# FFN output by seven products: three residual chunks loaded early, the last dual's sums in four parts

## The chip, the cores and the metric

The kernel runs on one core of a Trainium2 chip. The metric is the time of one execution on the device in microseconds. The times here are of that one core.

## The reference

One trunk layer on 1024 tokens of 1024 channels: a mixing sub-layer, then the feed-forward sub-layer (FFN), then a norm. The change lies in the FFN, where DFF is 2816:

```
h2 = rms_norm(x, norm_ffn_g[l]) * (1.0 + sc2) + sh2
a, bgate = jnp.split(jnp.einsum('bsd,df->bsf', h2, w_ffn_in[l]), 2, axis=-1)
x = x + g2 * jnp.einsum('bsf,fd->bsd', jax.nn.silu(a) * bgate, w_ffn_out[l])
...
return rms_norm(x, final_norm_g)
```

The product with `w_ffn_in` is called the FFN input below, the one with `w_ffn_out` the FFN output.

## The kernel before, in words

Activations are held transposed, channels on the 128 partitions and tokens along a row, in two halves of 512 tokens. Each float32 operand is split in a high part and the remainder (`th`, `tl` for activations, `wh`, `wl` for weights), and a product of two is three matmuls of 128x512 (`mm3`: lines 397, 398 and 400). A weight block lands in a `raw` buffer (line 218); ScalarE makes `wh` of it (line 234) and VectorE `wl` (line 235). There are three `wh` and three `wl` buffers, so that the cast for one product waits until TensorE is through with the product three places earlier. Of `raw` buffers there are six in this stage, in use in turn, and a load waits until the split of the block that lay there is done.

A 2x2 block product is made with seven products instead of eight (`PRODUCTS`, in the order 1, 2, 6, 5, 7, 3, 4). One such set of seven is called a **dual**. It needs sums of the four weight blocks (lines 254, 257, 259 and 301, on VectorE) and sums of the four blocks of the activation, and its results collect in three pairs of PSUM banks, x, y and z. In the z banks product 5 begins a sum, which is read out, and product 3 then adds to it.

The **FFN input** runs 11 duals. Each dual is followed by `hid_set`: from the four blocks of the activation it forms the seven operands of the FFN output, by four sums (lines 1336, 442, 1340 and 442), splits each in high and low (lines 437 on ScalarE and 438 on VectorE) and stores them to device memory. For the first ten duals they go through three `stage` buffers (line 1328), for the last dual through pairs of tiles called `hidh` and `hidl` (line 1324). Under each `in_product` of the last dual, `group_load` reads back the operands of group 0 for the product of the same number (line 1349), on the queue of GpSimd (POOL).

The **FFN output** takes the 11 operand sets in groups of 3, 4 and 4. For each group it runs two duals, d = 0 and d = 1, each for half of the output rows. A product of group 0 has 2 x 3 x 3 = 18 matmuls, one of groups 1 and 2 has 24. `out_evac` (line 1420, on VectorE) scales each bank and adds it to a chunk of the residual: chunk x1[j] holds 128 output channels of all tokens. Half d = 0 adds to chunks 0, 1, 4 and 5, half d = 1 to 2, 3, 6 and 7; the products 5, 7 and 4 to the later two of these (4 and 5, 6 and 7). The residual had been stored to device memory after the mixing sub-layer (`x1_dram`), and is loaded again: chunks 0 and 1 while the FFN input still runs, into buffers of their own (line 1408), the other six, in the order 4, 5, 2, 3, 6, 7, after the last dual's `hid_set` (line 1413), in the place that the `stage` buffers and the activation blocks (`gi`) held.

A scheduling layer sets the order of each engine's queue when the program is built, from the order of the code and its own estimate; on the chip each queue runs in order. DMAs of POOL's queue use eight semaphores in turn, so that each waits until the DMA eight places before it has landed.

Of the kernel before, what the change touches and what calls it, by code (L numbers as in the profile page):

```python
# [35 lines left out]
F32 = mybir.dt.float32  # L36
# [4 lines left out]
P = 128  # L41
D = 1024
T = 1024
H = 512
KC = D // P
# [86 lines left out]
def block_kernel(ctx: ExitStack, tc: tile.TileContext, x0, xT, c, vecs, ada, w_first, w_plain, w_duals,  # L132
                 w_short, w_conf, w_o, w_fi, w_fo0, w_fo1, outT):
    nc = tc.nc
# [4 lines left out]
    def open_pool(name, bufs, stack=None, **kw):  # L139

        p = tc.tile_pool(name=name, bufs=bufs, reuse_waits="tile", **kw)
        return p, (stack.enter_context(p) if stack else p.__enter__())

    def close(*pools):
        for p, _ in reversed(pools):
            p.__exit__(None, None, None)
# [27 lines left out]
    def g_tile(name):  # L174
        return gsp.tile([P, H], F32, tag="gs", name=name)
# [192 lines left out]
    def modulation(i, raw=None):  # L368

        if raw is None:  # L370
            raw = load(ada[i])
        else:
            nc.sync.dma_start(raw, ada[i])
        modulation_of(i, raw)
# [34 lines left out]
    def product(banks, m, t, evac=None, between=None, y_tile=ps2_tile, z_tile=ps_tile, onto=""):  # L409


        w = next_w()
        b = {"1": "x", "6": "x", "7": "x", "4": "x", "2": "y", "5": "z", "3": "z"}[m]
        n = len(t)
        for p in range(2):
            if (b, p) not in banks:
                banks[b, p] = {"x": ps_tile, "y": y_tile, "z": z_tile}[b](b)
            ps = banks[b, p]
            for k in range(n):
                c0 = (p * n + k) * P  # L420
                mm3([ps], slice(c0, c0 + P), w, [t[k]], m in "125" and m not in onto and k == 0, k == n - 1, m in "6734" + onto)
            if evac:
                evac(p, m, ps)
            if between and p == 0:
                between()
# [7 lines left out]
    def t_pair(name):  # L433
        return hl_tile(name + "h"), hl_tile(name + "l")

    def t_split(src, hi, lo):
        t_split.act = nc.scalar.copy(hi, src).ins  # L437
        t_split.ins = nc.vector.tensor_tensor(lo, src, f32(hi), ALU.subtract).ins  # L438

    def minus(out, a, b):  # L440

        nc.vector.scalar_tensor_tensor(out=out, in0=a, scalar=-1.0, in1=b, op0=ALU.mult, op1=ALU.subtract)
# [694 lines left out]
    for h in range(2):  # L1137
# [4 lines left out]
        for o in range(KC):  # L1142
            g = g_tile("gb")
# [9 lines left out]
    x1 = [None] * KC  # L1153
    x1_dram = [dram.tile([P, T], F32, name=f"x1_dram{j}") for j in range(KC)]
# [56 lines left out]
    def norm_2_sums(m):  # L1211

        b12, b22 = ([x1[k + i][:, halves[1]] for k in range(KH)] for i in (0, KH))
        b21 = [x1[k + KH][:, halves[0]] for k in range(KH)]
        with tc.issue_after(t_split.ins), tc.issue_after(t_split.act):
            for k in range(KH):
                if m == "7":
                    nc.vector.tensor_tensor(b12[k], b22[k], b12[k], ALU.subtract)
                elif m == "4":
                    minus(b21[k], t2[k], b21[k])  # L1220
            for k in range(KH):
                ts[m][k] = t_pair("t" + m)
                t_split({"5": x1[k][:, halves[0]], "7": b12[k], "3": b22[k], "4": b21[k]}[m], *ts[m][k])
        norm_2_sums.ins = t_split.ins

    N_IN = FC // 2
# [90 lines left out]
    def store(key, src):  # L1317

        hid_dram[key] = dram.tile([P, T], F32R, name="hid" + "_".join(map(str, key)))
        if key[0] == N_IN - 1:  # L1320
            hl = t_pair("hid")
            t_split(src, *hl)
            for t, s in zip(hl, halves):
                nc.gpsimd.dma_start(hid_dram[key][:, s], t)
            return
        s = stagep.tile([P, T], F32R, tag="stage", name="stage")
        t_split(src, s[:, :H], s[:, H:])
        nc.gpsimd.dma_start(hid_dram[key], s)  # L1328

    def hid_set(d):  # L1330

        (b11, b12), (b21, b22) = ((ha[2 * d + p, "4"], ha[2 * d + p, "6"]) for p in range(2))
        store((d, "1"), b11)
        store((d, "2"), b21)
        t2 = gip.tile([P, H], F32, tag="g", name="t2")
        nc.vector.tensor_tensor(b11, b11, b12, ALU.subtract)
        minus(t2, b11, b22)
        store((d, "6"), t2)
        store((d, "5"), b11)
        nc.vector.tensor_tensor(b12, b22, b12, ALU.subtract)  # L1340
        store((d, "7"), b12)
        store((d, "3"), b22)
        minus(b21, t2, b21)
        store((d, "4"), b21)

# [8 lines left out]
    def group_load(g, m):  # L1354
        to[g, m] = [t_load((FIRST[g] + i, m)) for i in range(GROUPS[g])]

    def in_product(d, m, between=None):
        late = EARLY[d] == 1
        if late and m == "2":
            for p in range(2):  # L1360
                in_evac(d)(p, "1", in_banks[d]["x", p])
        product(in_banks[d], m, ts[m], None if late and m == "1" else in_evac(d), between,
                z_tile=ps2_tile if d in (0, 2) else ps_tile)
        if d == N_IN - 1:
            group_load(0, m)
# [13 lines left out]
    for i, (d, m) in enumerate(in_order[5:]):  # L1379
        if i < 4:  # L1380
            norm_2_sums("5734"[i])
        elif i == 4:
            close(*phase_1)
            rawap = open_pool("raw_a", 1, side="right", stack=ctx)[1]
            raws.append(rawap)
            x1aps = [s2p, open_pool("x1a", 1, side="right", stack=ctx)[1]]
            phase_2 = [open_pool("gi", 7), open_pool("stage", 3, side="right")]
            gip, stagep = (p for _, p in phase_2)
        with ExitStack() as order:
            if d < 2:  # L1390
                order.enter_context(tc.issue_after(mm3.ins))
            in_product(d, m)
        if m == PRODUCTS[-1]:
            if 2 <= d < 6:
                with tc.issue_after(in_evac.ins):
                    for b in range(40 + 2 * (d - 2), 42 + 2 * (d - 2)):
                        modulation(b, x1aps[b % 2].tile([P, T], F32, tag="x1", name="ada"))
            if d:
                hid_set(d)
        elif (d, m) == (1, "6"):  # L1400
            hid_set(0)


    ng2 = cp.tile([P, KC], F32, name="ng2")
    nc.vector.tensor_scalar(ng2, mod[:, 40:48], -1.0, None, ALU.mult)
    x1 = [x1aps[j].tile([P, T], F32, tag="x1", name=f"x1{j}") for j in range(2)]
    for j in range(2):
        nc.gpsimd.dma_start(x1[j], x1_dram[j])
    close(*phase_2)
    x1bp = open_pool("x1b", 6, stack=ctx)[1]  # L1410
    x1 += [x1bp.tile([P, T], F32, tag="x1", name=f"x1{j}") for j in range(2, KC)]
    for j in (4, 5, 2, 3, 6, 7):
        nc.gpsimd.dma_start(x1[j], x1_dram[j])

    def out_evac(d):
        def evac(p, m, ps):
            low = m in "574"
            j = 2 * d + p + 4 * low
            dst = x1[j][:, halves[m in "6537"]]
            nc.vector.scalar_tensor_tensor(  # L1420
                out=dst, in0=ps, scalar=ng2[:, j : j + 1] if low else modc(40 + j), in1=dst, op0=ALU.mult, op1=ALU.add
            )
        return evac
# [43 lines left out]
    for g in range(FINAL):  # L1467
        for d in range(2):
            banks = {}
            for m in PRODUCTS:  # L1470
                product(banks, m, to[g, m], out_evac(d))
                if d == 0 and m == "1":
                    for q in PRODUCTS:
                        group_load(g + 1, q)

# [195 lines left out]
```

## Time and profile before

| | |
|---|---|
| median of 3 runs | 1468.83 us (1467.67 to 1469.37) |
| the profiled execution | 1467.46 us, of which its span is 1465.7 |
| TensorE (PE) busy | 1449.9 us, 99% of the span |
| VectorE (DVE) busy | 1187.2 us, 81% |
| ScalarE (ACT) busy | 628.1 us, 43% |
| GpSimd (POOL) busy | 517.3 us, 35% |
| moved by DMA | 257.68 MB, mean 176 GB/s |
| group 0 of the FFN output | 1236.90 to 1300.42 us of the span |

The last row is from the timeline of TensorE: the starts of the first matmul of group 0 and, counted from its last stretch, of group 1. In the profile a row of waits names the waiting engine and line, what released it, the us in total, how often, and the longest. In rows of the timeline an arrow reads "written from", and buffer numbers are left out; a wait for several things is put down to the one that came last. POOL's DMA rows show when a transfer was issued, not when it landed.

### The profile page before, as it was taken

The page shows a single profiled execution, that of the slowest core. Times are in us where ns is not written, and L with a number is a line of the kernel's source. Part 1 is how long each engine was busy: PE and PEld are TensorE (multiplying, and loading weights), DVE is VectorE, ACT ScalarE, POOL GpSimd, SP SyncE. Part 2 cuts the span into 40 slices and gives each one's busy share as a digit, 9 for nine tenths or more (in the row PEclk, how much of TensorE's full clock was granted, in tenths as well). Part 3 has the DMA queues.
Part 4 walks back from the last instruction along what each step waited for, and adds up shares of the span by engine and source line. Part 5 has one row for each costly group of instructions (what it writes and reads, how often), then busy time and mean ns, then how long its engine had stood idle before and what let it go on. Part 6 is the DMA issues. An engine that isn't in the chain of part 4 may idle for free.

```text
span 1465.7 us, 17716 instructions
## 1 busy us (share of the span) xinstructions
PE 1449.9 (99%) x6394; PEld 1188.9 (81%) x6394; DVE 1187.2 (81%) x1634; ACT 628.1 (43%) x911; POOL 517.3 (35%) x484
## 2 busy tenths in 40 slices
PE   9999999999999999999999999999999999899997
PEld 5888888888888888888888888888888888788887
DVE  8898999987988979999687798777777676766676
ACT  4873332334333337465226474444444443221235
POOL 0007777677677761111012001111111016642505
PEclk9999999999999999999999999999999999999999
DMA  9542232322222367486585336655554449994903
GB/s 372 185 149 73 73 101 72 115 72 101 72 87 72 129 216 259 134 269 197 198 314 202 107 121 227 226 186 188 176 173 147 145 146 358 393 357 136 363 4 116
DMA packets 88522, 257.68 MB, mean 176 GB/s; under 512 B 10177, under 2 KB 12865, under 8 KB 88434
## 3 DMA queue, kind: packets, MB, share of 16 engines
q1 hardware_dynamic: 43792, 142.04, 29.1%
q0 software_dynamic: 40608, 101.92, 21.1%
q10 hardware_dynamic: 4034, 12.59, 2.3%
q8 instruction: 50, 0.82, 0.2%
q14 instruction: 38, 0.31, 0.1%
HBM read 190.97 MB, written 65.54 MB: 175 GB/s over the span
## 4 chain that ended last, share of the span: by engine, by line
PE 83%; issue 2%; POOL 2%; DVE 2%; DMA 2%; ACT 0%; POOLq 0%; DVEq 0%; ACTq 0%
PE bank L400 11%; PE bank L398 11%; PE bank L397 11%; PE x L400 8%; PE x L398 8%; PE x L397 7%; PE z L397 3%; PE z L398 3%; PE z L400 3%; PE y L400 2%; PE y L398 2%; PE y L397 2%; PE mix L400 2%; PE mix L397 2%; PE yb L400 2%
## 5 line engine op out<-in xcount | busy, mean ns | idle before, releaser
L234 ACT CAST wh<-raw 128x1024 fp32r<-128x1024 f32 (+3 forms) x255 | 261.2, 1026 | 482.1 <-PE bank L398 153.6
L235 DVE TENSOR_TENSOR wl<-raw,wh 128x1024 fp32r<-128x1024 f32 (+3 forms) x176 | 208.9, 1188 | 50.5 <-ACT wh L234 47.9
L235 POOL TENSOR_TENSOR wl<-raw,wh 128x1024 fp32r<-128x1024 f32 x79 | 191.7, 2430 | 105.2 <-ACT wh L234 94.9
L972 DVE SCALAR_TENSOR_TENSOR c<-diff,vec,c 128x512 f32<-128x512 f32 x232 | 168.1, 750 | 2.7
L1328 POOL DMA_DIRECT2D hid<-stage x70 | 37.4, 535 | 343.6 <-DVE stage L438 340.2
L400 PE MATMUL bank<-th,wl 128*128 128x512 f32 x312 | 121.5, 389 | 0.5 <-POOL wl L235 0.5
L397 PE MATMUL bank<-th,wh 128*128 128x512 f32 x312 | 121.4, 389 | 0.0
L398 PE MATMUL bank<-tl,wh 128*128 128x512 f32 x312 | 121.4, 389 | 0.0
L972 DVE SCALAR_TENSOR_TENSOR c<-u,wsum,c 128x512 f32<-128x512 f32 x112 | 84.2, 752 | 2.3
L400 PE MATMUL x<-th,wl 128*128 128x512 f32 x176 | 68.6, 392 | 3.4 <-DVE wl L235 3.4
L397 PE MATMUL x<-th,wh 128*128 128x512 f32 x176 | 68.6, 390 | 0.7 <-ACT wh L234 0.7
L400 PEld LDWEIGHTS bank<-th,wl 128*128 128x128 f32 x312 | 58.6, 188 | 13.1 <-POOL wl L235 0.9
L398 PE MATMUL x<-tl,wh 128*128 128x512 f32 x176 | 68.7, 390 | 0.0
L398 PEld LDWEIGHTS bank<-tl,wh 128*128 128x128 f32 x312 | 58.6, 188 | 12.2
L397 PEld LDWEIGHTS bank<-th,wh 128*128 128x128 f32 x312 | 58.6, 188 | 12.2
L437 ACT CAST stage<-g 128x512 fp32r<-128x512 f32 x60 | 37.3, 622 | 67.9 <-DMA hid<-stage 45.3
L438 DVE TENSOR_TENSOR stage<-g,stage 128x512 fp32r<-128x512 f32 x60 | 41.2, 687 | 29.3 <-ACT stage L437 29.2
L1349 POOL DMA_DIRECT2D th<-hid x77 | 41.3, 536 | 60.1 <-PE x L400 37.0
L312 POOL TENSOR_TENSOR raw<-raw 128x1024 f32<-128x1024 f32 x8 | 20.8, 2605 | 108.6 <-DMA raw<-in_w_duals 104.6
L397 PE MATMUL yb<-zsh,wh 128*128 128x512 f32 x128 | 49.8, 389 | 0.0
L398 PE MATMUL yb<-zsl,wh 128*128 128x512 f32 x128 | 49.8, 389 | 0.0
L400 PE MATMUL yb<-zsh,wl 128*128 128x512 f32 x128 | 49.8, 389 | 0.0
(829 smaller groups left out, 4134.2 us busy)
## 6 DMA issues: line engine op xcount, KB each, us to landing
hid<-stage POOLq DMA_DIRECT2D x70, 512.0 KB, 4.7
raw<-in_w_duals SPq DMA_DIRECT2D x57, 512.0 KB, 3.5
raw<-in_w_fi SPq DMA_DIRECT2D x54, 512.0 KB, 4.0
th<-hid POOLq DMA_DIRECT2D x77, 256.0 KB, 5.9
tl<-hid POOLq DMA_DIRECT2D x77, 256.0 KB, 5.7
ada<-in_ada SPq DMA_DIRECT2D x24, 512.0 KB, 5.5
raw<-in_ada SPq DMA_DIRECT2D x24, 512.0 KB, 4.8
raw<-in_w_fo SPq DMA_DIRECT2D x16, 512.0 KB, 6.2
```

Source lines behind the costliest of these rows:

```text
L234: hi = nc.scalar.copy(wh, raw)
L235: lo = lo_engine.tensor_tensor(wl, raw, f32(wh), ALU.subtract)
L312: unit.eng.tensor_tensor(out, x, y, ALU.add)
L397: nc.tensor.matmul(ps, wh, xh, start=first, stop=False, skip_group_check=again)
L398: nc.tensor.matmul(ps, wh, xl, start=False, stop=False, skip_group_check=again)
L400: mm3.ins = nc.tensor.matmul(ps, wl, xh, start=False, stop=last, skip_group_check=again).ins
L437: t_split.act = nc.scalar.copy(hi, src).ins
L438: t_split.ins = nc.vector.tensor_tensor(lo, src, f32(hi), ALU.subtract).ins
L972: tap.ins = nc.vector.scalar_tensor_tensor(out=out, in0=src[:, s : s + H], scalar=wt, in1=acc, op0=ALU.mult, op1=ALU.add).ins
L1328: nc.gpsimd.dma_start(hid_dram[key], s)
L1349: nc.gpsimd.dma_start(t, hid_dram[key][:, s])
```

## The change

Three things are changed. `hid_set` becomes a generator with three stops, which cut the last dual's operands in four parts: 1 and 2; 6 and 5; 7 and 3; 4. The first part still follows the last dual at once. The other three are recorded behind products 1, 2 and 6 of the first half of group 0. For the other ten duals the parts follow one another as before.

After the last but one dual (number 9) its `stage` buffers are given back, three chunks x1[4], x1[5] and x1[2] take their place, and their loads are issued there. The chunks 3, 6 and 7 are loaded by `last_loads`, after the last part of the sums.

In group 0 the loads of group 1's operands are issued after product 6 of the first half instead of after product 1.

```diff
@@ hid_set
         store((d, "1"), b11)
         store((d, "2"), b21)
+        yield
         t2 = gip.tile([P, H], F32, tag="g", name="t2")
...
         store((d, "6"), t2)
         store((d, "5"), b11)
+        yield
         nc.vector.tensor_tensor(b12, b22, b12, ALU.subtract)
         store((d, "7"), b12)
         store((d, "3"), b22)
+        yield
         minus(b21, t2, b21)
         store((d, "4"), b21)
@@ the loop over the FFN input
-            if d:
-                hid_set(d)
+            last_set = hid_set(d)
+            if 0 < d < N_IN - 1:
+                list(last_set)
+            elif d:
+                next(last_set)
+            if d == N_IN - 2:
+                close(phase_2.pop())
+                x1bp = open_pool("x1b", 3, side="right", stack=ctx)[1]
+                x1 = {j: (x1aps[j] if j < 2 else x1bp).tile([P, T], F32, tag="x1", name=f"x1{j}") for j in (0, 1, 4, 5, 2)}
+                for j in x1:
+                    nc.gpsimd.dma_start(x1[j], x1_dram[j])
         elif (d, m) == (1, "6"):
-            hid_set(0)
+            list(hid_set(0))
@@ between FFN input and output
-    x1 = [x1aps[j].tile([P, T], F32, tag="x1", name=f"x1{j}") for j in range(2)]
-    for j in range(2):
-        nc.gpsimd.dma_start(x1[j], x1_dram[j])
-    close(*phase_2)
-    x1bp = open_pool("x1b", 6, stack=ctx)[1]
-    x1 += [x1bp.tile([P, T], F32, tag="x1", name=f"x1{j}") for j in range(2, KC)]
-    for j in (4, 5, 2, 3, 6, 7):
-        nc.gpsimd.dma_start(x1[j], x1_dram[j])
+    def last_loads():
+        close(*phase_2)
+        x1cp = open_pool("x1c", 3, stack=ctx)[1]
+        for j in (3, 6, 7):
+            x1[j] = x1cp.tile([P, T], F32, tag="x1", name=f"x1{j}")
+            nc.gpsimd.dma_start(x1[j], x1_dram[j])
@@ the loop over the FFN output
                 product(banks, m, to[g, m], out_evac(d))
-                if d == 0 and m == "1":
+                if (g, d) == (0, 0) and m in "126":
+                    next(last_set, None)
+                    if m == "6":
+                        last_loads()
+                if d == 0 and m == ("1" if g else "6"):
                     for q in PRODUCTS:
                         group_load(g + 1, q)
```

The scheduling layer's order moves in three places that matter below. Number suffixes differ between the two builds; lines 1336, 1340, 1349 and 1420 of before are 1337, 1342, 1352 and 1432 now.

On POOL's queue, at the last `stage` store of dual 9 and the first loads of group 0's operands (`hid_2_7112` is operand 2 of dual 0), before:

```order
L1328 DMA hid_4_9582<-stage 128x1024
L1349 DMA th<-hid_2_7112 128x512
L1349 DMA tl<-hid_2_7112 128x512
L1349 DMA th<-hid_2_7298 128x512
L1349 DMA tl<-hid_2_7298 128x512
L1349 DMA th<-hid_2_7553 128x512
```

and now:

```order
L1328 DMA hid_4_9582<-stage 128x1024
L1352 DMA th<-hid_2_7112 128x512
L1352 DMA tl<-hid_2_7112 128x512
L1352 DMA th<-hid_2_7298 128x512
L1411 DMA x_9593<-x_dram_5891 128x1024
L1411 DMA x_9594<-x_dram_5892 128x1024
L1411 DMA x_9595<-x_dram_5889 128x1024
L1352 DMA tl<-hid_2_7298 128x512
L1352 DMA th<-hid_2_7553 128x512
```

The three chunks 4, 5 and 2 stand there ahead of 33 operand loads; before, they stood behind these and behind the 14 stores of the last dual.

On VectorE, from the weight split of product 3 of the first half (`wl_10187`, now `wl_10190`) to the first weight sum of the second half (line 254), before:

```order
L235 TENSOR_TENSOR wl_10187<-raw_9979,wh_10186 128x768
L438 TENSOR_TENSOR hidl_9947<-g4_9883,hidh_9946 128x512
L235 TENSOR_TENSOR wl_10213<-raw_9983,wh_10212 128x768
L254 TENSOR_TENSOR raw_10292<-raw_10240,raw_10242 128x768
L257 TENSOR_TENSOR raw_10240<-raw_10240,raw_10236 128x768
L235 TENSOR_TENSOR wl_10245<-raw_10236,wh_10244 128x768
L1420 TENSOR_SCALAR x14_9965<-z_10190,ng2_9952,x14_9965 128x512
```

and now, from the same split up to the second evacuation of product 7:

```order
L235 TENSOR_TENSOR wl_10190<-raw_9932,wh_10189 128x768
L438 TENSOR_TENSOR hidl_9988<-g4_9882,hidh_9987 128x512
L1432 TENSOR_SCALAR x14_9593<-z_10193,ng2_9926,x14_9593 128x512
L438 TENSOR_TENSOR hidl_10022<-g6_9711,hidh_10021 128x512
L1432 TENSOR_SCALAR x15_9594<-z_10204,ng2_9926,x15_9594 128x512
L438 TENSOR_TENSOR hidl_10029<-g6_9725,hidh_10028 128x512
L235 TENSOR_TENSOR wl_10216<-raw_9936,wh_10215 128x768
L438 TENSOR_TENSOR hidl_10061<-g4_9897,hidh_10060 128x512
L1432 TENSOR_SCALAR x14_9593<-x_9954,ng2_9926,x14_9593 128x512
L1432 TENSOR_SCALAR x15_9594<-x_9965,ng2_9926,x15_9594 128x512
```

Product 5's evacuations (`x14<-z`) stood behind the weight sum of line 254 and the weight split of the second half's product 1; now they stand ahead of both, between the splits of the last dual's operands. Line 254 now stands five rows below the last one shown, behind a weight split, both evacuations of product 3 and another weight split.

On TensorE, behind the last matmul of product 7 of the first half (bank `x_10012`, now `x_9965`), before:

```order
L400 MATMUL x_10012<-th_9812,wl_10162 128x512
L397 MATMUL x_10300<-th_9625,wh_10244 128x512
L398 MATMUL x_10300<-tl_9626,wh_10244 128x512
L397 MATMUL x_10311<-th_9625,wh_10244 128x512
L398 MATMUL x_10311<-tl_9626,wh_10244 128x512
L400 MATMUL x_10300<-th_9625,wl_10245 128x512
```

and now:

```order
L400 MATMUL x_9965<-th_9826,wl_10035 128x512
L397 MATMUL z_10193<-th_9858,wh_10189 128x512
L398 MATMUL z_10193<-tl_9859,wh_10189 128x512
L400 MATMUL z_10193<-th_9858,wl_10190 128x512
L397 MATMUL z_10193<-th_9862,wh_10189 128x512
```

Before, eight matmuls of the second half's product 1 (bank `x_10300` and `x_10311`) stood ahead of product 3; now product 3 follows product 7 directly, and product 1 of the second half comes after product 4.

## The prediction

> **What bounds the kernel now.** I read the page first, for which engine fills the span; then the waits of the tensor engine, for where it isn't filled; then the stretch in which they fall, engine by engine.
>
> ```profile
> span 1465.7 us, 17716 instructions
> PE 1449.9 (99%) x6394; PEld 1188.9 (81%) x6394; DVE 1187.2 (81%) x1634; ACT 628.1 (43%) x911; POOL 517.3 (35%) x484
> PE x L400 <- DVE wl L235: 3.4, 1, 3.4
> PE x L397 <- ACT wh L234: 0.7, 1, 0.7
> ```
>
> TensorE is busy for 99% of the span, and the change removes no matmul, so it can only gain what TensorE loses. The two rows of waits (engine, line, releaser, total us, times, longest) are the only ones between 1200 and 1420 us, and they are neighbours (rows of the timeline: start, length, engine, line, what, and in brackets the wait before):
>
> ```profile
> 1257.07 0.39 PE L400 MATMUL x<-th,wl 128*128 128x512 f32 x1
> 1258.20 0.50 PE L397 MATMUL x<-th,wh 128*128 128x512 f32 x1 [0.74 <-ACT wh L234]
> ...
> 1259.00 0.39 PE L398 MATMUL x<-tl,wh 128*128 128x512 f32 x1
> 1262.84 0.50 PE L400 MATMUL x<-th,wl 128*128 128x512 f32 x1 [3.45 <-DVE wl L235]
> ...
> 1264.19 0.63 PE L397 MATMUL z<-th,wh 128*128 128x512 f32 x1
> ```
>
> Busy time by stretch (columns: length, then busy us of PE, PEld, DVE, ACT, POOL with counts, granted clock, DMA share, GB/s) gives the price:
>
> ```profile
> 1236.90:1257.30 20.40, 20.40 (x91) 16.70 (x89) 15.83 (x23) 9.91 (x15) 12.66 (x24) 1.00 1.18 374
> 1257.30:1262.84 5.54, 1.35 (x6) 0.68 (x5) 2.85 (x4) 0.83 (x1) 3.35 (x8) 1.00 1.12 412
> 1262.84:1275.94 13.10, 13.10 (x51) 10.65 (x51) 9.53 (x13) 1.67 (x2) 7.64 (x15) 0.87 1.16 403
> 1275.94:1300.42 24.48, 24.48 (x110) 20.27 (x108) 16.86 (x21) 5.46 (x6) 15.70 (x31) 1.00 1.19 393
> ```
>
> I set the borders at matmul starts. The first stretch is the first five products of group 0's first half, 90 matmuls by the program's order: 20.40 / 90 = 0.2267 us each. The last is 108 matmuls in 24.48 us, the same. Between them stand 54 matmuls, which at that pace take 12.24 us and took 5.54 + 13.10 = 18.64. The hole costs **6.40 us**: 4.50 of it as gaps (0.90 ahead of 1258.20, 3.61 ahead of 1262.84, beyond the pace), the rest, 1.9, as matmuls at the 0.87 mean clock behind them (0.63 us in place of 0.39).
>
> Here a rule of the Trainium skill can be weighed. "TensorE: Matmul & The Clock Gate", Part 1, says that after an idle window of about 3.4 us the clock falls to half until about 3.4 us of work. By that rule a 3.45 us wait costs near 1.7 us on top (my estimate from the page: half of one window), and a 0.74 us wait nothing. The trace agrees, with 1.9 and with a normal 0.39 us matmul after the short wait. The sum doesn't hang on it, since the measured hole holds both.
>
> Who made the hole? VectorE's own rows:
>
> ```profile
> 1252.75 0.95 DVE L235 TENSOR_TENSOR wl<-raw,wh 128x768 fp32r<-128x768 f32 x1
> 1253.62 0.68 DVE L438 TENSOR_TENSOR hidl<-g,hidh 128x512 fp32r<-128x512 f32 x1
> 1254.22 0.95 DVE L235 TENSOR_TENSOR wl<-raw,wh 128x768 fp32r<-128x768 f32 x1
> 1259.96 0.96 DVE L254 TENSOR_TENSOR raw<-raw 128x768 f32<-128x768 f32 x1 [4.79 <-DMA raw<-in_w_fo]
> ...
> 1261.83 0.95 DVE L235 TENSOR_TENSOR wl<-raw,wh 128x768 fp32r<-128x768 f32 x1
> 1262.70 0.75 DVE L1420 SCALAR_TENSOR_TENSOR x<-z,ng,x 128x512 f32<-128x512 f32 x1
> ```
>
> VectorE runs in order and stood 4.79 us ahead of the weight sum L254, for a weight block. Behind it was queued the low half of the weights (1261.83) for which TensorE waited. Two places on stood product "5"'s evacuation into x1[4] (1262.70), without which product "3" may not add to the z banks. That evacuation had its own late input:
>
> ```profile
> 1214.67 0.54 POOL L1328 DMA_DIRECT2D hid<-stage  x1 [1.27 <-DVE stage L438]
> ...
> 1216.26 0.56 POOL L1349 DMA_DIRECT2D th<-hid  x1
> 1216.78 0.56 POOL L1349 DMA_DIRECT2D tl<-hid  x1
> ...
> 1221.69 0.53 POOL L1349 DMA_DIRECT2D tl<-hid  x1 [1.40 <-DMA hid<-stage]
> ...
> 1225.20 0.53 POOL L1349 DMA_DIRECT2D tl<-hid  x1 [0.71 <-PE x L400]
> ...
> 1237.90 0.53 POOL L1349 DMA_DIRECT2D tl<-hid  x1 [0.18 <-issue]
> ...
> 1242.64 0.55 POOL L1349 DMA_DIRECT2D tl<-hid  x1
> ...
> 1254.59 0.53 POOL L1324 DMA_DIRECT2D hid<-hidl  x1 [0.21 <-DMA raw<-in_w_fo]
> 1255.47 0.54 POOL L1413 DMA_DIRECT2D x<-x_dram  x1 [0.34 <-DMA hid<-hidl]
> ...
> 1261.14 0.54 POOL L1349 DMA_DIRECT2D th<-hid  x1 [0.17 <-issue]
> ...
> 1307.52 0.53 POOL L1349 DMA_DIRECT2D tl<-hid  x1
> ```
>
> ```profile
> DMA to landing us min/median/max: 6.9/7.6/8.8
> 1253.76 0.33 SPq L218 DMA_DIRECT2D raw<-in_w_fo  x1
> raw<-in_w_fo SPq DMA_DIRECT2D x7, 384.0 KB, 6.0
> th<-hid POOLq DMA_DIRECT2D x43, 256.0 KB, 5.9
> ```
>
> The x1[4] load went out at 1255.47 and needs 6.9 us at least (first row here: the six x1 loads): 1262.4. The weight block went out at 1253.76, when the split of 1252.75 had freed its buffer, and landed for 1259.96. So there are **two covers**, of like length: without either one the other would still hold TensorE most of the way.
>
> **The change, part by part.** (1) *x1[4], x1[5], x1[2] early.* They stand behind the `th` load of 1216.26. The first waits for the last stage buffer's store of 1214.67, which the trace shows landed at 1221.69 (a load waited on it there). Landing by 1221.7 + 8.8 = 1230.5, they are 21 us ahead of product "5"'s evacuation. That cover goes whole.
>
> What they push is POOL's queue. Behind them stand 33 loads for group 0. Four of those went out in the 4.9 us up to 1221.69; with three chunks of twice their size that makes 10 units of 256 KB. At 374 GB/s (first stretch) a unit takes 0.70 us, so the rest goes out up to **7.0 us later**; at the 412 GB/s of the second stretch, 6.4. The last, issued at 1242.64, goes out by 1249.6 and lands, with 5.9, by 1255.5. Its product "4" starts at 1236.90 + 6 x 18 x 0.2267 = 1261.38. That leaves 5.9 us. For product "3" (last load 1237.90, start 1257.30) the same count leaves 6.5, for "6" (1225.20, 1245.06) 7.0. I take this at 0; the loads' lead hides it, and each us beyond that lead would cost one.
>
> (2) *Sums of the last dual in four parts.* No work is added: seven splits, four sums, 14 stores, but VectorE's order changes. Each instruction starts this long after the one before, from these rows: an L438 split 0.61, an evacuation 0.66, a weight split 0.87 (1252.75 to 1253.62 above). The sums are of the same 128x512 size, and I give them the split's.
>
> ```profile
> 1249.62 0.68 DVE L438 TENSOR_TENSOR hidl<-g,hidh 128x512 fp32r<-128x512 f32 x1
> 1250.23 0.74 DVE L1420 SCALAR_TENSOR_TENSOR x<-x,mod,x 128x512 f32<-128x512 f32 x1
> 1250.89 0.68 DVE L438 TENSOR_TENSOR hidl<-g,hidh 128x512 fp32r<-128x512 f32 x1
> ...
> 1284.10 0.39 PE L397 MATMUL z<-th,wh 128*128 128x512 f32 x1
> ...
> 1286.34 0.75 DVE L1420 SCALAR_TENSOR_TENSOR x<-z,ng,x 128x512 f32<-128x512 f32 x1 [0.42 <-PE z L400]
> ```
>
> An evacuation can start 2.24 us after its product (1284.10 to 1286.34). Product "6" starts at 1245.06, so VectorE begins the new chain at 1247.30: evacuation, two splits, one sum, evacuation, three sums, a split, the weight split of "3", a split. That is 2 x 0.66 + 8 x 0.61 + 0.87 = 7.1 us, so that "3"'s weights are there at 1253.8 (needed at 1257.30) and "5"'s first evacuation runs from 1254.4 to 1255.1. It is needed at 1257.30: **2.2 us to spare**, the tightest place, and I cost it at 0. The chain goes on without gaps (two splits and "5"'s other evacuation, "4"'s weight split, a split, two evacuations, then the weight split of the next product) to 1260.6, where the latter is wanted at 1265.46.
>
> (3) *L254 stands later.* It now follows both evacuations of "3" (the second can start at 1257.30 + 2.04 + 2.24 = 1261.58) and one weight split, so it starts near 1263.2. Its weight block is freed by "3"'s split (ended 1253.8) and lands with 6.0 at 1259.8: 3.4 us of cover in place of 4.79 us of waiting. From L254 to the next weights are three sums, two evacuations, one sum and one split, 5.9 us: 1269.1, against the product's start at 1273.62.
>
> (4) *Group 1's loads after product "6"; x1[3], x1[6], x1[7] behind the last stores.* Those stores follow the last split, near 1258.3 (before: 1254.59), so the three loads go out near 1259.5 and land by 1268.3; x1[3] is due at 1269.7. Group 1's loads start near 1262 instead of 1261.14. Their last went out at 1307.52 and serves the product that starts at 1300.42 + 6 x 24 x 0.2267 = 1333.1; with TensorE 6.4 us earlier and 5.9 to landing, 12 us are left. Cost 0.
>
> Sum: the profiled execution took 1467.46 us (span 1465.7 and 1.76 around it). 1467.46 - 6.40 = **1461.1**. The median of the three timed runs is 1468.83, 1.37 higher, and no row says whether that lies in the hole; I put the forecast half way, at **1461.8**.
>
> **The rivals.** *A: the hole shrinks but stays.* The chain of (2) slips by more than its 2.2 us: each store step waits for ScalarE's high half, and ScalarE casts in order between weight casts. VectorE's 15.83 of 20.40 us busy says that it is dense; ScalarE's 9.91 speaks against. A slip of 4 us leaves TensorE 1.8 us of wait, under the 3.45 that was followed by a slow clock: some 1463.6, and 1466 at the worst with one slow stretch.
>
> *B: it doesn't do what it says.* The block for L254 lands so late that VectorE stands there again, with product "6" of the second half behind it. That needs a landing 4.5 + 3.4 us later than worked out, some 14 us after issue, where the longest landing in these rows is 8.8. For the whole hole to come back it must be 20. Time: 1466 to 1468.8.
>
> *C: slower.* One mechanism: POOL's queue. The three chunks stand ahead of 33 operand loads while the DMA engines are full (share 1.12 to 1.19). Once the delay exceeds the lead, products "7", "3" and "4" wait for operands. With 7.0 us worked out and some 6 left, it decides from about 13 us on, and to lose more than the hole gives it must reach 19.5; at 22 the time is some 1471. That would need the queue to stand some 15 us at the wait for the stage buffer, which was over at 1221.69. The Trainium skill speaks for this rival ("DMA: Bandwidth & Descriptors", Issuing engines are not separate DMA queues): all queues run on the same 16 engines and interleave, so a load moved earlier makes others later. The trace agrees, with the 374 to 412 GB/s that no stretch here exceeds; the lead decides.
>
> **How the numbers follow.** The forecast has 0.82, A 0.08, B 0.05, C 0.05. About 0.2% (2.9 us) can be told from no change: faster means under 1465.9. The forecast and nearly all of A lie there, B mostly not. The range begins at 1459.9, 1.2 us under the sum, for a hole that is that much longer in other executions, and ends at 1465.5, over most of A; B, C and A's worst are left out, some 0.13.
>
> **What would show it.** In the profile after: no wait of TensorE over 0.3 us between 1200 and 1420 and a granted clock of 1.00 there; group 1's first product near 1294.0; VectorE without a wait at L254; the first x1[4] load issued near 1221.7; the last group 0 load near 1249. A wait of TensorE for `th` shows C, for VectorE at "3" A, at the second half's "6" B. What would make it wrong most simply is a wait that I have not ordered: an engine's queue in which one late input holds an instruction that needs none.

## The result, and the profile after

The changed kernel takes **1461.86 us** (median of 5 runs, 1460.76 to 1462.86); beside it the kernel before took 1468.83 us (5 runs, 1467.67 to 1469.37). The ratio is 0.9953, with a 95% interval of 0.9938 to 0.9967: faster, by 7 us.

The first lines of the page of after: its span, and the busy time of each engine.

```profile
span 1459.9 us, 17713 instructions
PE 1447.7 (99%) x6394; PEld 1188.2 (81%) x6394; DVE 1184.7 (81%) x1634; ACT 627.9 (43%) x911; POOL 514.7 (35%) x484
```

The view of TensorE's waits has no row left between 1200 and 1420 us. The stretches with the borders of the prediction (columns as there):

```profile
1236.90:1257.30 20.40, 20.40 (x92) 16.90 (x91) 15.59 (x23) 9.91 (x15) 13.63 (x27) 1.00 1.20 391
1257.30:1262.84 5.54, 5.54 (x26) 4.61 (x25) 5.19 (x8) 1.63 (x2) 2.84 (x6) 1.00 1.22 400
1262.84:1275.94 13.10, 13.10 (x60) 10.84 (x59) 11.36 (x15) 2.56 (x4) 8.05 (x16) 1.00 1.14 374
1275.94:1300.42 24.48, 24.48 (x110) 20.28 (x109) 17.67 (x22) 5.12 (x6) 15.02 (x29) 1.00 1.20 385
```

In the second row TensorE was busy for 1.35 of 5.54 us and is so for all of it now; in the third the granted clock is 1.00 where it was 0.87. The hole is gone. Group 1's first product starts at 1294.67, 1294.0 by before's clock (less 0.65, see below), as forecast.

The span fell by 5.8 us only, and the hole was 6.4. The rest is the start: the first matmul of group 0 (timeline of TensorE) stands 0.65 us later in this execution, and TensorE has no wait from 1200 us up to there, in either kernel.

```profile
1237.55 0.39 PE L397 MATMUL x<-th,wh 128*128 128x512 f32 x1
```

In the executions of this study that moment lies anywhere between 1236.4 and 1239.6 us. So I compare profiles by their **tail**: the span less the start of group 0. Before it is 1465.7 - 1236.90 = 228.80 us, after 1459.9 - 1237.55 = 222.35: **6.45 us** less, where the prediction's sum said 6.40. Times of after that are set beside predicted ones below are lessened by 0.65.

VectorE after, from the weight split of "3" to the next weights (timeline):

```profile
1253.49 0.95 DVE L235 TENSOR_TENSOR wl<-raw,wh 128x768 fp32r<-128x768 f32 x1
1254.36 0.68 DVE L438 TENSOR_TENSOR hidl<-g,hidh 128x512 fp32r<-128x512 f32 x1
1254.96 0.74 DVE L1432 SCALAR_TENSOR_TENSOR x<-z,ng,x 128x512 f32<-128x512 f32 x1
...
1263.79 0.95 DVE L254 TENSOR_TENSOR raw<-raw 128x768 f32<-128x768 f32 x1
...
1268.91 0.96 DVE L235 TENSOR_TENSOR wl<-raw,wh 128x768 fp32r<-128x768 f32 x1
```

No bracket stands at L254: its wait of 4.79 us is gone. Product 5's evacuation (L1432) starts at 1254.96, ahead of it. POOL after (timeline):

```profile
1222.13 1.57 POOL L1411 DMA_DIRECT2D x<-x_dram  x3 [5.01 <-issue]
...
1249.87 0.53 POOL L1352 DMA_DIRECT2D tl<-hid  x1 [1.11 <-PE x L398]
...
1261.88 0.53 POOL L1324 DMA_DIRECT2D hid<-hidh  x1 [2.34 <-DMA hid<-hidh]
...
1263.49 1.58 POOL L1425 DMA_DIRECT2D x<-x_dram  x3 [0.55 <-issue]
...
1268.90 0.53 POOL L1352 DMA_DIRECT2D tl<-hid  x1 [1.13 <-DMA x<-x_dram]
```

The three chunks go out together at 1222.13, the last operand load of group 0 at 1249.87, the other three chunks behind the last stores at 1263.49. The last row waits, eight DMAs behind x1[3], until that has landed: 1268.90.

### The profile page after: what moved, and what is told of

Read it like the earlier page. It is cut to its first block, busy times and chain, and to the rows that moved or that the text cites. A ratio compares the mean times of both kernels' runs of the same rounds, so it can differ in the third digit from the quotient of the medians.

```text
span 1459.9 us, 17713 instructions
## 1 busy us (share of the span) xinstructions
PE 1447.7 (99%) x6394; PEld 1188.2 (81%) x6394; DVE 1184.7 (81%) x1634; ACT 627.9 (43%) x911; POOL 514.7 (35%) x484
## 4 chain that ended last, share of the span: by engine, by line
PE 87%; POOL 2%; DVE 1%; issue 1%; DMA 0%; POOLq 0%; ACT 0%
PE bank L400 11%; PE bank L397 11%; PE bank L398 11%; PE x L398 8%; PE x L400 8%; PE x L397 8%; PE z L397 4%; PE z L400 4%; PE z L398 4%; PE y L400 2%; PE y L398 2%; PE y L397 2%; PE mix L400 2%; PE yb L400 2%; PE mix L398 2%; PE yb L398 2%
```

## The experiments

My theory was that of two covers: before, product 3 was held twice over, by VectorE's wait at the weight sum L254 (the order of its queue) and by the late chunk x1[4], and either one alone would have held TensorE most of the way. The rivals: that one of the two was idle cover all along, and that the operand loads pay for the early chunks. All seven runs in one table; the gain or loss against after is that of the tails. A tail is that of one execution, the profiled one; in e5_queue_3, e5_queue_6 and e8_chain_3 that was the slowest or the second slowest, 1.3 to 3.0 us above the median, in e4_sums_ahead one 1.7 us below it.

| kernel | median us (runs) | ratio to before, 95% | span | group 0 starts | tail | against after |
|---|---|---|---|---|---|---|
| before | 1468.83 (5) | | 1465.7 | 1236.90 | 228.80 | +6.45 |
| after | 1461.86 (5) | 0.9953 (0.9938 to 0.9967) | 1459.9 | 1237.55 | 222.35 | 0 |
| e1_early_only | 1462.20 (5) | 0.9954 (0.9942 to 0.9967) | 1460.4 | 1238.04 | 222.36 | +0.01 |
| e2_parts_only | 1461.40 (5) | 0.9952 (0.9938 to 0.9965) | 1459.5 | 1237.11 | 222.39 | +0.04 |
| e4_sums_ahead | 1467.30 (11) | 0.9990 (0.9982 to 0.9999) | 1463.8 | 1236.39 | 227.41 | +5.06 |
| e6_order_only | 1467.82 (11) | 0.9995 (0.9986 to 1.0004) | 1465.8 | 1236.46 | 229.34 | +6.99 |
| e5_queue_3 | 1463.49 (6) | 0.9966 (0.9954 to 0.9978) | 1464.8 | 1239.64 | 225.16 | +2.81 |
| e5_queue_6 | 1466.82 (11) | 0.9989 (0.9980 to 0.9997) | 1466.5 | 1238.86 | 227.64 | +5.29 |
| e8_chain_3 | 1463.36 (5) | 0.9967 (0.9955 to 0.9980) | 1462.8 | 1239.19 | 223.61 | +1.26 |

The kernel before, run beside the first four experiments, took 1468.54 us (median of 21 runs), beside the last three 1468.35 (16).

### The early loads alone

To the kernel before, one edit:

```diff
+            if d == N_IN - 2:
+                close(phase_2.pop())
+                x1bp = open_pool("x1b", 3, side="right", stack=ctx)[1]
+                x1 = {j: (x1aps[j] if j < 2 else x1bp).tile([P, T], F32, tag="x1", name=f"x1{j}") for j in (0, 1, 4, 5, 2)}
+                for j in x1:
+                    nc.gpsimd.dma_start(x1[j], x1_dram[j])
...
-    x1bp = open_pool("x1b", 6, stack=ctx)[1]
...
-    for j in (4, 5, 2, 3, 6, 7):
+    x1cp = open_pool("x1c", 3, stack=ctx)[1]
+    for j in (3, 6, 7):
...
```

> The kernel before, with one edit alone: chunks 4, 5 and 2 are loaded behind dual 9, in the place of the stage buffers. The last dual's sums stay undivided and the loads of group 1 stay behind product 1. Theory: the late chunks alone made the scheduling layer set product 5's evacuations behind the weight sum, so that the early loads alone bring VectorE's new order and take away both covers: 1461 to 1463 us, no wait of TensorE over 0.3 us between 1200 and 1420 us, no wait of VectorE at the weight sum. Rival, as my prediction had it: the order changes because the sums come in four parts, so that here VectorE still stands some 4.8 us at the weight sum and TensorE loses 5 to 6.4 us: 1466 to 1469 us.

The theory holds, and **the rival, my own, falls**: 1462.20 us, with the tail of after to 0.01 us. VectorE's order is that of after, without the four parts (timeline of VectorE, e1_early_only):

```profile
1253.97 0.96 DVE L235 TENSOR_TENSOR wl<-raw,wh 128x768 fp32r<-128x768 f32 x1
1254.84 0.69 DVE L438 TENSOR_TENSOR hidl<-g,hidh 128x512 fp32r<-128x512 f32 x1
1255.44 0.75 DVE L1423 SCALAR_TENSOR_TENSOR x<-z,ng,x 128x512 f32<-128x512 f32 x1
...
1264.28 0.95 DVE L254 TENSOR_TENSOR raw<-raw 128x768 f32<-128x768 f32 x1
```

With the chunk late the scheduling layer put the evacuation behind the weight sum; with the chunk early it comes first. That the layer's estimate of when the chunk is there decides this is my reading; the runs show the orders only. One edit thus takes away both covers, and the cut in four parts adds nothing to it.

### The parts alone

To the changed kernel:

```diff
-                for j in x1:
+                for j in range(2):
                     nc.gpsimd.dma_start(x1[j], x1_dram[j])
...
         close(*phase_2)
+        for j in (4, 5, 2):
+            nc.gpsimd.dma_start(x1[j], x1_dram[j])
```

The three chunks keep the place of the `stage` buffers, which is free from dual 9 on; so this is not the kernel before with the cut alone.

> The changed kernel, with chunks 4, 5 and 2 loaded between the last dual's stores, as late as before, while the four parts and the place of group 1's loads stay. Theory of the late chunk: x1[4] goes out near 1250.5 to 1251.5 us and lands with 5.5 to 6.9 us near 1256 to 1258.4, and x1[5] later still, where product 5's evacuations run at 1254.4 to 1255.6 in the changed kernel; product 3 may not start at 1258 but follows 2 us behind the landing of x1[5], so TensorE waits 1 to 6 us at product 3: 1463 to 1468 us. Rival: the four parts and the order of VectorE are what took the hole away, and the chunk's time hardly counts: 1461 to 1462.5 us.

1461.40 us, and no wait of TensorE: the rival's time, and my expectation missed. I had expected the loads near 1251 us; they went out earlier, among the stores (POOL and VectorE, e2_parts_only):

```profile
1243.95 0.53 POOL L1423 DMA_DIRECT2D x<-x_dram  x1 [0.30 <-DMA tl<-hid]
...
1248.72 0.54 POOL L1423 DMA_DIRECT2D x<-x_dram  x1
...
1257.06 0.53 POOL L1324 DMA_DIRECT2D hid<-hidh  x1 [0.74 <-DMA x<-x_dram]
```

```profile
1254.43 0.75 DVE L1434 SCALAR_TENSOR_TENSOR x<-z,ng,x 128x512 f32<-128x512 f32 x1
1256.63 0.75 DVE L1434 SCALAR_TENSOR_TENSOR x<-z,ng,x 128x512 f32<-128x512 f32 x1 [1.45 <-PE x L400]
...
1261.33 0.96 DVE L254 TENSOR_TENSOR raw<-raw 128x768 f32<-128x768 f32 x1 [2.42 <-DMA raw<-in_w_fo]
```

x1[4] at 1243.95, 11.5 us ahead of before, was in time for 1254.43. x1[5], sent at 1248.72, was late for VectorE: the second evacuation stood 1.45 us for it (the row names TensorE, which had long been done; the store eight places behind x1[5] found it landed by 1257.06). But product 3, started at 1237.11 + 90 x 0.2267 = 1257.51, reaches that bank nine matmuls, or 2.04 us, later, so that some 2 us were left. The chunks never came late enough to put the theory to the test, and the run doesn't refute that a late chunk holds TensorE; it says that the place before the 33 operand loads is far earlier than needed. VectorE still stands 2.42 us at L254, with product 5's evacuations ahead of it, and that costs nothing: **it is what stands behind the wait, not the wait, that cost.**

### The order of before, with early chunks

In the changed kernel the second half's first two weight sums are made in a step of their own (`ahead`, lines 287 and 288, the work of lines 254 and 257), and product 5's evacuations are held behind them:

```diff
+                if (g, d, m) == (0, 0, "5"):
+                    sums_5.append(ahead_of[0, 1]["ahead"]())
                 product(banks, m, to[g, m], out_evac(d))
...
+            with tc.issue_after(sums_5[0]) if sums_5 and (d, m) == (0, "5") else ExitStack():
```

> The changed kernel with early chunks, but the first two weight sums of the second half stand ahead of product 5's two evacuations on VectorE, as they did before the change. Theory of two covers: VectorE stands there 4 to 5 us for the last weight block of the second half, which is loaded into a buffer that the split of product 3 frees near 1254 us and lands near 1260; product 5's evacuations and with them product 3 come 5 to 6 us late, though the chunks have long landed: TensorE waits 3 to 5 us, its clock falls behind it, 1466 to 1469 us. Rival: only the late chunk held TensorE before, and the sum's wait was hidden: 1461 to 1462.5 us.

1467.30 us: most of the hole is back, though the three chunks went out at 1220.12 us. VectorE, then TensorE (e4_sums_ahead):

```profile
1259.06 0.96 DVE L287 TENSOR_TENSOR raw<-raw 128x768 f32<-128x768 f32 x1 [2.49 <-DMA raw<-in_w_fo]
1259.93 0.95 DVE L235 TENSOR_TENSOR wl<-raw,wh 128x768 fp32r<-128x768 f32 x1
1260.80 0.95 DVE L288 TENSOR_TENSOR raw<-raw 128x768 f32<-128x768 f32 x1
1261.67 1.40 DVE L1446 SCALAR_TENSOR_TENSOR x<-z,ng,x 128x512 f32<-128x512 f32 x2
```

```profile
1257.69 0.50 PE L410 MATMUL x<-th,wh 128*128 128x512 f32 x1 [0.74 <-ACT wh L234]
...
1260.94 0.50 PE L413 MATMUL x<-th,wl 128*128 128x512 f32 x1 [2.06 <-DVE wl L235]
...
1261.51 0.58 PE L411 MATMUL x<-tl,wh 128*128 128x512 f32 x1
1261.88 0.63 PE L413 MATMUL x<-th,wl 128*128 128x512 f32 x1
```

The same two waits as before, here of 0.74 and 2.06 us (before: 0.74 and 3.45), and a slow clock behind them: 5.06 us in the tail. The waits are shorter than I expected, because in this execution the sum stood for 2.49 us and not for 4.79. The first cover is shown by itself.

### The order of after, with late chunks

In the kernel before, the weight sums of group 0's second half are held behind product 3's evacuations:

```diff
-                sums("132", after)
+                with tc.issue_after(behind_3.pop(0)) if n == 768 and behind_3 else ExitStack():
+                    sums("132", after)
...
+            if (d, m) == (0, "3"):
+                behind_3[:] = [ins]
```

> The kernel before, with the late chunks, but the weight sums of the second half of group 0 stand behind product 3's evacuations on VectorE, as they do after the change. Theory of two covers: product 5's evacuation now waits for x1[4] itself, issued near 1255.5 us and landed at 1262.4 at the earliest, so that product 3 starts near 1263.5 in place of 1257.3: TensorE waits 4 to 6 us, its clock falls behind it, and product 1 of the second half no longer has matmuls ahead of product 3 to fill the gap: 1466 to 1470 us. Rival: the wait at the weight sum alone held TensorE, and the chunk lands in time for it: 1461 to 1463 us.

1467.82 us, in the tail 6.99 us worse than after. POOL, VectorE and TensorE (e6_order_only):

```profile
1255.76 0.53 POOL L1416 DMA_DIRECT2D x<-x_dram  x1 [0.66 <-DMA hid<-hidl]
```

```profile
1263.58 0.75 DVE L1423 SCALAR_TENSOR_TENSOR x<-z,ng,x 128x512 f32<-128x512 f32 x1 [4.88 <-DMA x<-x_dram]
```

```profile
1264.39 0.58 PE L400 MATMUL z<-th,wh 128*128 128x512 f32 x1 [3.97 <-DVE x L1423]
1264.77 0.63 PE L401 MATMUL z<-tl,wh 128*128 128x512 f32 x1
```

With the sum out of the way the evacuation waits for the chunk itself, 4.88 us, until 1263.58 (worked out: 1262.4 at the earliest); TensorE starts product 3 at 1264.39, and the clock falls. The second cover is shown too. In the kernel before, the two ended together. The load eight places behind x1[4]'s waited there until that had landed (POOL, before):

```profile
1262.76 0.53 POOL L1349 DMA_DIRECT2D th<-hid  x1 [0.45 <-DMA x<-x_dram]
```

The evacuation behind the weight sum started at 1262.70 (the prediction shows its row). Neither wait outlasted the other, so that taking away either gains next to nothing.

One clause of the expectation was wrong: ten matmuls of the second half's product 1 still stand ahead of product 3 on TensorE. So they do in each kernel with the hole (eight before, twelve in e4_sums_ahead), and in none of after, e1_early_only and e2_parts_only. The 0.74 us wait for ScalarE's cast comes with them; before, it is 0.90 + 0.10 of the 6.40 us (ahead of 1258.20 and behind it). What TensorE's order costs by itself wasn't tried.

### More load in POOL's queue

In the changed kernel the three early loads are issued two times (e5_queue_3) or three times (e5_queue_6, with `[:9]` in place of `[:6]`):

```diff
-                for j in x1:
+                for j in (0, 1) + ((4, 5, 2) * 5)[:6]:
                     nc.gpsimd.dma_start(x1[j], x1_dram[j])
```

> The changed kernel, with the loads of chunks 4, 5 and 2 issued a second time behind the first, so that POOL's queue carries three useless transfers of 512 KB ahead of the 33 operand loads (the data stay the same). Each second load waits until the first into its buffer has landed, some 6 us after 1222, so that the operand loads start near 1231 us in place of 1223.7: a dose of some 7 us. In the changed kernel's trace the last load of group 0 was issued at 1249.87 us, lands with the median of 6.0 us near 1255.9, and its product starts at 1262.0: a lead of 6.2 us. If the lead hides a delay up to its own size and no more, and the loads catch up none of it: TensorE waits 0 to 2 us in group 0, 1461 to 1465 us. If part of the dose is caught up on the way: 1461 to 1462.5. Rival: the full DMA engines already delay the operands, and every us of queue costs one: 1468 to 1470 us.

> As before with the same loads issued three times, so that two rounds of useless transfers stand ahead of the 33 operand loads: a dose of some 13.5 us. If the lead of 6.2 us decides and nothing is caught up: TensorE waits 7 to 8 us in all for operands in group 0, with one or two stretches of slow clock behind it: 1468 to 1472 us, as slow as the kernel before or slower. If the loads catch up most of the dose: 1461 to 1465 us. If every us of queue costs one: 1475 us.

**e5_queue_3**: 1463.49 us, tail +2.81. The last operand load went out at 1257.84; after's, moved by the two starts (2.09), at 1251.96. Those 5.9 us cost nothing in group 0's first half, as the lead said. The loss came elsewhere (e5_queue_3; the last operand load, the late chunks, VectorE in front of x1[3], TensorE):

```profile
1257.84 0.53 POOL L1352 DMA_DIRECT2D tl<-hid  x1
1269.83 1.61 POOL L1425 DMA_DIRECT2D x<-x_dram  x3
```

```profile
1275.77 0.75 DVE L1432 SCALAR_TENSOR_TENSOR x<-x,mod,x 128x512 f32<-128x512 f32 x1 [3.71 <-DMA x<-x_dram]
1276.44 0.95 DVE L259 TENSOR_TENSOR raw<-raw 128x768 f32<-128x768 f32 x1
```

```profile
PE x L397 <- ACT wh L234: 1.9, 1, 1.9
PE x L400 <- DVE wl L235: 0.3, 1, 0.3
```

The delayed queue delays the stores behind it and with them x1[3]; VectorE stands in front of that chunk with the next weight sum (L259) queued behind, and TensorE waits for those weights. It is the old pattern one chunk further on, and again with an order of its own: in after, L259 and the split behind it (1268.91) stand ahead of x1[3]'s evacuation. So the 2.81 us are the price of a later chunk and of a worse order together.

**e5_queue_6**: 1466.82 us, tail +5.29. The last operand load goes out at 1264.04, which is 12.9 us later than after's (moved by 1.31). Now TensorE waits for operands, as rival C had it (waits of TensorE):

```profile
PE x L398 <- DMA tl<-hid: 1.4, 2, 0.8
PE z L397 <- DMA th<-hid: 0.5, 1, 0.5
PE x L397 <- DVE x L1432: 0.4, 1, 0.4
PE x L397 <- DMA th<-hid: 0.2, 1, 0.2
```

The median lies between what was expected with the dose caught up (1461 to 1465 us) and without (1468 to 1472). By TensorE's timeline the waits for operands and the pace lost beside them cost 4.2 us, at products 2, 6, 5 and 7 of the first half; products 3 and 4, whose loads go out last, didn't wait, since TensorE was that much later itself by then; so the lead at the last load isn't what decided. Another 0.7 us go at an evacuation of the second half (the third row). No wait was longer than 0.8 us, and the granted clock stayed at 1.00. The rival "every us costs one" is excluded by both: 5.9 and 12.9 us of delay cost 2.81 and 5.29.

### The spare time ahead of product 5's evacuation

In the changed kernel:

```diff
+            if (d, m) == (0, "5") and len(more) == 1:
+                for _ in range(3):
+                    with tc.issue_after(more[-1]):
+                        more.append(nc.vector.tensor_tensor(x1[2][:, :H], x1[2][:, :H], x1[2][:, :H], ALU.max).ins)
+            with tc.issue_after(more[-1]) if len(more) > 1 and (d, m) == (0, "5") else ExitStack():
...
```

> The changed kernel, with three useless VectorE instructions (the maximum of half of chunk 2 with itself, which changes nothing) set ahead of product 5's evacuations. Together with three splits that the scheduling layer now puts among them they move the first evacuation back by some 3.7 us, from 1255.0 to 1258.6. In the changed kernel's trace it ended at 1255.7 and product 3 started at 1257.96: 2.25 us to spare. Four matmuls of the second half now stand ahead of product 3 and fill 0.9 us. If the spare time is what I read: product 3 starts near 1259.4 and TensorE loses 0.5 to 1.5 us, 1462.3 to 1463.5 us. Rival: the evacuation isn't what product 3 waits for: 1461.9 and no wait. Rival: a delay here is multiplied, since the weight splits and the clock behind it are late too: above 1465 us.

1463.36 us, tail +1.26: the size that the first theory gave, but not by its wait. VectorE and TensorE (e8_chain_3):

```profile
1260.21 1.40 DVE L1437 SCALAR_TENSOR_TENSOR x<-z,ng,x 128x512 f32<-128x512 f32 x2
```

```profile
1260.49 0.50 PE L397 MATMUL x<-th,wh 128*128 128x512 f32 x1 [0.74 <-ACT wh L234]
...
1261.52 0.40 PE L397 MATMUL z<-th,wh 128*128 128x512 f32 x1
```

The evacuations start at 1260.21 (1258.57 by after's clock, 1258.6 worked out). Product 3 starts at 1261.52, right behind the four matmuls of the second half's product 1 (from 1260.49) and without a wait. In e6_order_only product 3 followed 0.81 us behind the start of its evacuation (1263.58 to 1264.39); here that would be 1261.02, so the evacuation was in time. Of the 1.26 us TensorE lost 1.0 in group 0, 0.90 ahead of 1260.49 and 0.10 behind it, and all of that to ScalarE's cast of the weights of those four matmuls. ScalarE, first e8_chain_3, then after:

```profile
1259.61 0.83 ACT L234 CAST wh<-raw 128x768 fp32r<-128x768 f32 x1 [1.68 <-issue]
```

```profile
1257.97 0.84 ACT L234 CAST wh<-raw 128x768 fp32r<-128x768 f32 x1 [1.68 <-issue]
```

1259.61 less 1.64 is 1257.97: the cast is no later than in after, where products 3 and 4 stand ahead of the matmuls that need it. The expectation let the four matmuls fill 0.9 us and left out that their weights aren't there yet. So the size came out by luck. The spare time of 2.25 us stays a reading of after, which this run doesn't test, and whether product 3 would have had to wait isn't shown either; that it does wait for this evacuation when that is later still, e6_order_only shows. The second rival, a delay that multiplies, is out: 1463.36 us, and a granted clock of 1.00 here.

## Why the prediction was right, and where it was not

**The sum.** 6.40 us of hole were to go; the tail lost 6.45. The medians differ by 6.97. That the other executions of before were slower than the profiled one, and that half of this might lie in the hole, was a choice without a row. It came out (1461.8 against 1461.86), but no run shows why, and the interval of the ratio, 4.8 to 9.1 us, is far wider than that: the last tenths are luck.

**Two covers: right.** With either one alone 5 to 7 us of the gain are lost again (e4_sums_ahead, e6_order_only); the kernel that has lost only one cover gains 0.1% over before or less (ratios 0.9990 and 0.9995). The prediction counts the wait for ScalarE's cast, 0.90 us, in the hole, and doesn't say that it goes with TensorE's own order.

**Step 1, right.** The chunks were to go out near 1221.7 and did at 1222.13 (1221.5 by before's clock); the last operand load by 1249.6, and it did at 1249.2. The lead of some 6 us covers that: 5.9 us more cost no operand wait, 12.9 did.

**Step 2: the times right, the cause wrong.** The evacuation was worked out for 1254.4 and came at 1254.3; it ended at 1255.7 in after, where product 3 started at 1257.96: 2.25 us to spare, where 2.2 was said. But the step ("No work is added ... but VectorE's order changes") laid VectorE's new order to the cut in four parts. e1_early_only has the order and the time without the cut. The order had followed from step 1. The two orders show all edits together, and I gave each edit a share of the difference. With the cut and the chunks' buffers free from dual 9 on, loads recorded as late as the last stores do too (e2_parts_only); whether the cut alone would do, with the chunks in their old place, wasn't run.

**Step 3, right.** L254 was to start near 1263.2 without a wait, the next weights to be there at 1269.1; L254 started at 1263.1 and the split of those weights ran from 1268.3 to 1269.2.

**Step 4: no cost, as said, but mis-sized.** The three late chunks were to go out near 1259.5; they did at 1262.8 by before's clock. I let the stores follow the last split, and left out that each waits for the DMA eight places before it: the store at 1261.88 stood 2.34 us for that. x1[3] landed at 1268.90 (1268.3 by before's clock, as said) because its load took 5.4 us where I had allowed 8.8: two errors that cancel. Its evacuation is the second of a pair that starts at 1269.79, so at some 1270.45: **1.5 us to spare**, less than the 2.2 that I had called the tightest place, and the step's own figures (1268.3 and 1269.7) had left only 1.4. e5_queue_3 shows what lies behind a later x1[3], there with another order of VectorE: 2.81 us. The new place of group 1's loads wasn't taken back by itself in the changed kernel; in e1_early_only these loads stand behind product 1, and the time is the same.

**Rival C: right in kind, too dear in price.** It was to start at a delay of 13 us and to eat the hole at 19.5. The change's own delay, worked out as 7.0 us, measured 6.6 (the last operand load at 1242.64 before, 1249.2 now by before's clock). It starts to cost earlier, through x1[3] and not through the operands: 4 to 6 us more already cost 2.8. And it costs less: at 6.6 + 12.9 = 19.5 us, where it was to eat the whole hole, 5.29 are lost, and e5_queue_6 is as fast as before or a little faster. The operands waited for were those of products 2, 6, 5 and 7, not of 7, 3 and 4.

## What to carry to other kernels

Where an engine waits, list what else its next instructions need, and when that arrives: a wait can cover a second one of like length, and then only what takes both gains anything. Where a layer sets the order, a late load can come with a worse order on other engines, so build each edit alone before giving it the credit. When a run gives the time that was expected, look whether the wait is the expected one too. When a load is moved forward, look for the least spare time behind it in the same queue to the end, not only at the transfers directly behind it.

## What was unexpected of the hardware

The clock fell after a shorter wait than the 3.45 us of the kernel before. In e4_sums_ahead the longest wait is 2.06 us, with 0.74 us shortly before, and the granted clock was 0.51 from 1261.51 to 1264.87 (columns as in the result):

```profile
1256.79:1261.51 4.72, 1.93 (x8) 1.16 (x7) 2.46 (x3) 0.83 (x1) 2.68 (x6) 1.00 1.23 401
1261.51:1264.87 3.36, 3.36 (x9) 2.59 (x8) 3.36 (x6) 0.00 (x0) 3.19 (x7) 0.51 1.22 368
```

In e5_queue_3 a wait of 1.86 us with 0.26 behind it was followed by no fall. The Trainium skill, "TensorE: Matmul & The Clock Gate", Part 1, has the clock fall after at least one idle window of about 3.4 us. Here TensorE was idle for 2.8 of 4.7 us, with eight matmuls among them and no single wait over 2.06 us, so one unbroken idle stretch of that length was not needed. Where the limit lies between e4_sums_ahead and e5_queue_3 wasn't tried. The slow stretch itself lasted 3.4 us here and 3.4 in e6_order_only (1264.39 to 1267.76), which agrees with the Trainium skill, "TensorE: Matmul & The Clock Gate", Part 1, where about 3.4 us of sustained work bring the clock back.

The other surprise is how far group 0's start moves between executions, 1236.4 to 1239.6 us, 1.64 us apart in after and e8_chain_3, whose code is alike up to there. Part of it is there long before: the first store of the residual starts at 737.8 us in after and at 739.3 in e5_queue_3. That is up to half of the effect measured, and the spans of two profiles can't be compared without taking it out.
